# A hybrid decoder step on one core: sample queries, first q/k transposes and softmax steps in other places of the program

## The chip, the core and the metric

The kernel runs on one core of a Trainium2 chip: TensorE (PE in the profile, with PEld for its weight loads), VectorE (DVE), ScalarE (ACT), GpSimd (POOL) and SyncE (SP, which issues most of the DMAs). The metric is the device time of one execution in microseconds (us). Before the change the median of three timed runs is 905.75 us (904.86 to 906.82).

## The reference, cut to what matters

One decoder layer is computed for a prompt of 512 tokens and for 8 samples of one new token each; every sample has 4096 past tokens in a paged cache of 32 pages of 128 tokens. All is in float32.

```python
z = rmsnorm(x, attn_norm_w) @ w_in             # -> q latent, kv latent, rope key, u, v
q = (rmsnorm(q_lat, q_norm_w) @ w_uq).reshape(B, T, 8, 96)
q_nope, q_rope = rmsnorm(q[..., :64]), rope(rmsnorm(q[..., 64:]))
k_nope = rmsnorm(einsum('bkr,rhd->bkhd', c, w_uk), k_nope_norm_w)   # also for every cached token
s = (q_nope . k_nope + q_rope . k_rope) * SCALE                    # causal
o = softmax(s) @ c @ w_uv
u, v = gelu(z_u), gelu(z_v)
sg = u * (tril(w_s) @ v + b_s)                 # per chunk of 128 tokens, 8 groups
h = x + concat([o, sg]) @ w_o
h = h + conv_ffn(rmsnorm(h));  h = h + sigmoid(rmsnorm(h) @ w_ple_gate) * e
```

The normalisation of a cached key needs the sum of squares of its 64 values, so for every page the product `c @ w_uk` (128 tokens by 8 heads by 64) is really computed; the scores of the sample's query come out of the same matmul in 8 more columns (`w_uk` has 2 x 256 columns and 2 x 4 more, which hold the query folded through `w_uk`).

## The kernel before

Nearly all products are float32 in three passes (`mm3`, lines 149 to 151): each operand is split into a high part in a short format (a copy or cast, L138 or L140, on ACT, at times on POOL) and the rest (a subtraction, L133 or L146, on DVE or POOL), and high x high, high x rest and rest x high are added up in PSUM.

The order in which an engine issues its instructions is drawn up when the kernel is built: a scheduler takes them in the order of the program, by what it believes to be ready at each moment, so that a later instruction can stand ahead of an earlier one that it believes to be still waiting. On the chip each engine then keeps that order strictly. `with tc.issue_after(x.ins)` makes the instructions of a block stand behind instruction `x` on its engine. Tiles come from pools with few buffers: `ms` (2 banks of PSUM), `mm` (3 pairs of banks), `G` (10), `A` (8), `W` (9), `WR` (3), `U` (20), and a new tile waits until an old one of its pool has been read for the last time.

The stages, with the times of the profiled execution:

- 0 to 76 us: input norm, the projections to q, kv and u. For each of five token tiles (four of the prompt, t = 0 to 3, and t = 4 with the 8 samples) q and k are normalised and q's 32 rope columns are turned (L470 to L473 and `rope`, L373 to L376), in the order t = 4, 0, 1 on DVE and t = 2, 3 on POOL.
- 76 to 119 us: the products with `w_v` for the five tiles (`v_mm`, 24 matmuls of 512 columns each, order 4, 0, 1, 2, 3), each followed by the gelu on ACT (L520), and the chunk mixing (`mix`): for a prompt tile the split of v, 12 matmuls against the lower-triangular `w_s` (`wsh`, `wsl`, made from `wsr` by L883 and a split), four additions on DVE (L563) and four products on POOL (L567); for the samples' tile two operations on DVE (L542, L543), four small transposes on TensorE (L546) and four products (L548). Into this stage the scheduler has put: the samples' queries: 8 transposes (L484), a scaling (L485), ACT copies into the block-diagonal `qbd` (L506), 8 matmuls through `w_ukT` (L500), the score of the new token (L486 to L494, on 8 partitions of DVE); and the transposes of q and k of the first two prompt heads (L645, four at a time, `t_step`), whose results are split into `G` and `A` tiles.
- 119 to 206 us: attention of the prompt in 16 blocks (`pa_score`, `pa_t`, `pa_out`), with two cache pages of sample 0 in each block.
- 206 to 408 us: the pages of samples 1 to 7. `s_page` takes one page: 6 matmuls of 260 columns in an `mm` tile, the square on ACT (L761), the copy of the raw scores on ACT (L762) and the sum of squares on DVE (L763). Four pages form a group n (n = 0 to 63, eight to a sample); a group is loaded by SP (L605), its rope keys gathered by POOL (L592), and it is split on ACT or POOL (L719) and POOL (L133) two or three groups ahead. The softmax of sample b runs as small `steps` behind given pages of sample b+1. The gated mixture `sgr` is split in four parts behind the groups in `SGS`, high part on ACT, rest on POOL.
- 408 to 906 us: output projection (`o_half`), the convolutional FFN, the gate.

The steps of the softmax before, by the page that they stand behind: 4: variance (L804) and its logarithm; 5: exponential, square; 6: L815; 7: L160 and L161; 8: L817; 9: the maximum (L818); 16: its transpose (L794); 17: L797 and L798; 20: L801, which spreads the maximum by a matmul; 21 to 24: subtraction, exponential, sum; 27: the product with the cached latents (L838); 29: its copy.

Of the kernel before, what the change touches and what calls it, by code (L numbers as in the profile page):

```python
# [7 lines left out]
F32 = mybir.dt.float32  # L8
# [4 lines left out]
AF = mybir.ActivationFunctionType  # L13
# [9 lines left out]
DN = 64  # L23
# [16 lines left out]
NG = 10  # L40
NAT = 8
KRQ = 4
SGS = (51, 54, 59, 62)
EF = 3
PF = 2

# [2 lines left out]
def trunk_step(ctx: ExitStack, tc: tile.TileContext, I, O):  # L49
# [98 lines left out]
    def mm3(out, lh, ll, rh, rl, start, stop):  # L148
        nc.tensor.matmul(out, lh, rh, start=start, stop=False)  # L149
        nc.tensor.matmul(out, lh, rl, start=False, stop=False)  # L150
        return nc.tensor.matmul(out, ll, rh, start=False, stop=stop)  # L151
# [275 lines left out]
    def h96(t, n=128):  # L427
        return t[:n, 0:768].rearrange("p (h d) -> p h d", d=DQ)
# [50 lines left out]

    qs_, ks_ = qtok[4], ktok[4]  # L480
    qgT = const([96, 8, 8], F32, "qgT")
    ps = ms()
    for h in range(8):
        nc.tensor.transpose(ps[:96, h * 8:h * 8 + 8], qs_[:8, h * DQ:(h + 1) * DQ], ident[:8, :8])  # L484
    nc.vector.tensor_scalar(qgT.rearrange("p h b -> p (h b)"), ps[:96, 0:64], gq96[:, 0:1], None, op0=ALU.mult)  # L485
    nc.vector.tensor_mul(h96(ks_, 8)[:, :, 0:DN], h96(ks_, 8)[:, :, 0:DN], gqk8[:, 0:1].to_broadcast([8, 8, DN]))  # L486
    nc.vector.tensor_mul(qs_[:8, 0:768], qs_[:8, 0:768], ks_[:8, 0:768])
    snew = S()
    nc.vector.tensor_reduce(snew[:8, 0:8], h96(qs_, 8), axis=AX.X, op=ALU.add)
    nc.vector.tensor_scalar(snew[:8, 0:8], snew[:8, 0:8], SCALE, None, op0=ALU.mult)  # L490
    snall = const([128, 8, 8], F32, "snall")
    nc.gpsimd.memset(snall, NEG)
    nc.vector.tensor_mul(snall[:8], eye8[:, 0].rearrange("p (b h) -> p b h", b=8), snew[:8, 0:8].unsqueeze(1).to_broadcast([8, 8, 8]))
    nc.vector.tensor_add(snall[:8], snall[:8], eye8[:, 1].rearrange("p (b h) -> p b h", b=8))  # L494

    wukT = WR()
    nc.sync.dma_start(wukT[0:64, 0:1024], I["w_ukT"])
    ps = ms()
    for h in range(8):
        nc.tensor.matmul(ps[:, h * 8:h * 8 + 8], wukT[0:64, h * 128:(h + 1) * 128], qgT[0:64, h], start=True, stop=True)  # L500
    qtil = const([128, 8, 8], F32, "qtil")
    nc.vector.tensor_copy(qtil.rearrange("p h b -> p (h b)"), ps[:, 0:64])
    qbd = const([128, 8, 4, 8], F32, "qbd")
    nc.gpsimd.memset(qbd, 0.0)
    for j in range(4):
        nc.scalar.copy(qbd[32 * j:32 * j + 32, :, j, :], qgT[64:96].rearrange("p h b -> p b h"))  # L506


    bsb = G()
# [7 lines left out]
    def v_out(t, ps):  # L517
        n = TOK[t][1]
        vg[t] = G()
        nc.scalar.activation(vg[t][:n, 0:512], ps, AF.Gelu_apprx_tanh, scale=rtok[:n, t:t + 1])  # L520

    def v_mm(t):
        t0, n = TOK[t]
        sl = slice(t0, t0 + n)
        ps = mm()[:n, 0]
        for j in range(4):
            wh, wl = wget(k_v[j], 3 - j)
            for i in range(2):
                mm3(ps, xh[j][:, i, sl], xl[j][:, i, sl], u3(wh, 2, 512)[:, i], u3(wl, 2, 512)[:, i],
                    j == 0 and i == 0, j == 3 and i == 1)  # L530
        v_out(t, ps)

    def mix(t):
        t0, n = TOK[t]
# [87 lines left out]

    pq_ = {}

    def prep_items(hp):

        qk = [None] * 4
        pq_[hp] = [None, qk]

        def v_step():  # L630
            cs = slice(hp * 128, hp * 128 + 128)
            ps = ms()
            for t in range(4):
                ts_ = slice(t * 128, t * 128 + 128)
                nc.tensor.matmul(ps[:, ts_], ct[:, ts_], wuv[:, cs], start=True, stop=True)
            v = G()
            nc.scalar.copy(v[:, 0:512], ps)
            pq_[hp][0] = v

        def t_step(c, w):  # L640
            h = 2 * hp + c
            src, sc = ((qtok, gq96), (ktok, None))[w]
            ps = ms()
            for t in range(4):
                nc.tensor.transpose(ps[:96, t * 128:(t + 1) * 128], src[t][:, h * DQ:(h + 1) * DQ], ident)  # L645
            th, tl = (A(F32R), A(F32R)) if c else (G(F32R), G(F32R))
            split(th[:96, 0:512], tl[:96, 0:512], ps[:96], scale=None if sc is None else sc[:, 0:1])
            qk[2 * c + w] = (th, tl)

        return [lambda: t_step(0, 0), lambda: t_step(0, 1), lambda: t_step(1, 0), lambda: t_step(1, 1), v_step]  # L650
# [57 lines left out]
    def s_split(n):  # L708
        if n >= 64:
            return  # L710
        b, g = n // 8, n % 8
        pv = pages[b][1][g]
        if n < 12:
            t = U(F32R)
            ch, cl = t[:, 0:512], t[:, 512:1024]
        else:
            ch, cl = A(F32R)[:, 0:512], A(F32R)[:, 0:512]
        raw = pv[:, :, 0:128]
        (nc.gpsimd.tensor_copy if n % 2 else nc.scalar.copy)(u3(ch, 4, 128), raw)  # L719
        subs.append(sub(u3(cl, 4, 128), raw, u3(ch, 4, 128), "g"))  # L720
        csp[n] = (ch, cl)
# [48 lines left out]
    def s_softmax(b):  # L770

        ss, raw, scp = bst[b]
        sc = scp[:, 0:264]
        s3 = sc.rearrange("p (c h) -> p c h", h=8)
        yt = G()
        y0, t = yt[:, 0:256], yt[:, 256:512]
        m1, m2, psum = S(), S(), S()

        def act(*args, **kw):
            with tc.issue_after(squares[-1].ins):  # L780
                exps.append(nc.scalar.activation(*args, **kw))

        bst[b] = (scp, psum)
        hold = {}

        def after_keys(f):

            with tc.issue_after(kmms[-1].ins):
                f()

        def mx_t(after=None):
            hold["t"] = ms()
            with tc.issue_after((after or kmms[-1]).ins):
                nc.tensor.transpose(hold["t"][:8, 0:128], m1[:, 0:8], ident)  # L794

        def mx_all():
            nc.vector.tensor_reduce(m2[:8, 0:1], hold["t"][:8, 0:128], axis=AX.X, op=ALU.max)  # L797
            nc.vector.tensor_scalar(m2[:8, 8:16], ident[:8, 0:8], m2[:8, 0:1], None, op0=ALU.mult)  # L798

        def mx_b():  # L800
            after_keys(lambda: nc.tensor.matmul(hold["t"][:, 128:136], ones[:8], m2[:8, 8:16], start=True, stop=True))  # L801

        def var():
            nc.gpsimd.tensor_scalar(ss, ss, 1.0 / DN, EPS, op0=ALU.mult, op1=ALU.add)  # L804
            act(y0, ss, AF.Ln)

        def rstd():
            act(y0, y0, AF.Exp, scale=-0.5)
            act(t, y0, AF.Square)

        with_qbd[16] = mx_t
        steps.update({
            4: var,
            5: rstd,
            6: lambda: nc.vector.tensor_mul(raw, raw, y0),  # L815
            7: lambda: newton(raw, ss, raw, t),
            8: lambda: nc.vector.tensor_add(sc[:, 0:256], sc[:, 0:256], raw),  # L817
            9: lambda: nc.vector.tensor_reduce(m1[:, 0:8], s3.rearrange("p c h -> p h c"), axis=AX.X, op=ALU.max),  # L818
            17: mx_all,
            20: mx_b,  # L820
            21: lambda: nc.vector.tensor_sub(s3, s3, hold["t"][:, 128:136].unsqueeze(1).to_broadcast([128, 33, 8])),
            23: lambda: act(sc, sc, AF.Exp),
            24: lambda: nc.vector.tensor_reduce(psum[:, 0:8], s3.rearrange("p c h -> p h c"), axis=AX.X, op=ALU.add),
            27: lambda: s_pv(b),
            29: lambda: s_out(b),
        })
# [58 lines left out]
    split(wsh[:, 0:1024], wsl[:, 0:1024], wsr[:, 0:1024])  # L885
    v_mm(0)
    mix(4)
    p0 = prep_items(0)
    p0 = prep_items(0)
    v_mm(1)  # L890
    mix(0)
    p0[0]()
    v_mm(2)
    mix(1)
    p0[1]()
    p0[2]()
    v_mm(3)
    tc.keep_in_program_order(nc.scalar.preload_act_table_set("natural_log_exp_and_others"))
    wuv = G()
    nc.sync.dma_start(wuv[:, 0:512], I["w_uv"])  # L900
    s_load(0)
    s_split(0)
    s_split(1)
    mix(2)
    mix(3)
    p0[3]()
    p0[4]()
    blocks = [(hp, qb) for hp in range(4) for qb in range(4)]
    pa_score(0, 0)
# [360 lines left out]
```

## Time and profile before

| what | us |
|---|---|
| median of three timed runs | 905.75 |
| lowest, highest | 904.86, 906.82 |
| the profiled execution, device time | 907.9 |
| its span in the trace | 906.0 |

The mean granted TensorE clock over the span is 0.989. A page of the profile lists busy times of the engines, then groups of instructions; the timeline lists instructions by start and duration with what ended the idle time before them; the table of waits sums such idle times by who waited for whom; the table of stretches gives busy time and granted clock of chosen intervals. Durations of matmuls overlap, so the start of the next one tells how long one costs.

### The profile page before, as it was taken

How to read it: one execution, taken by the hardware profiler on the slowest of the kernel's cores; microseconds unless marked ns; L12 is line 12 of the kernel's file. 1: busy time of each engine (PE TensorE's matmuls, PEld its weight loads, DVE VectorE, ACT ScalarE, POOL GpSimd, SP SyncE). 2: the span in 40 equal slices, each digit the busy share in tenths (PEclk: the TensorE clock that was granted, in tenths of full speed). 3: DMA queues.
4: the chain of work that ended last, by engine and by line, in shares of the span. 5: the costliest groups of instructions: out<-in, count | busy, mean ns of one | idle time of the engine just before them, and what ended most of it. 6: DMA issues, size and time to landing. Idle time of an engine off the chain costs nothing.

```text
span 906.0 us, 20621 instructions
## 1 busy us (share of the span) xinstructions
PE 884.8 (98%) x7847; PEld 843.4 (93%) x7847; DVE 645.2 (71%) x1093; ACT 503.6 (56%) x1182; POOL 215.0 (24%) x243
## 2 busy tenths in 40 slices
PE   8998999999999999999999999999999999999997
PEld 6896878889999999889999999999999999999997
DVE  6579676668888898796669776337775437766774
ACT  6573368778888888784446443124443224455561
POOL 4004851237777777730000000000000000000000
PEclk9999999999999999999999999999999999999999
DMA  6332160243667664613332222322222322323311
GB/s 220 99 97 82 48 186 1 80 137 98 180 186 214 190 194 135 203 59 110 84 122 88 89 88 75 113 94 94 94 93 71 116 94 83 97 84 100 117 59 60
DMA packets 65347, 100.43 MB, mean 111 GB/s; under 512 B 13841, under 2 KB 47770, under 8 KB 65250
## 3 DMA queue, kind: packets, MB, share of 16 engines
q1 hardware_dynamic: 63202, 94.93, 33.2%
q0 software_dynamic: 2048, 4.20, 1.8%
q8 instruction: 62, 1.02, 0.5%
q14 instruction: 35, 0.29, 0.1%
HBM read 95.95 MB, written 3.15 MB: 109 GB/s over the span
## 4 chain that ended last, share of the span: by engine, by line
PE 77%; DVE 7%; ACT 6%; issue 4%; DMA 3%; SPq 3%; POOL 1%; ACTq 0%; POOLq 0%; DVEq 0%
PE mm L149 23%; PE mm L150 23%; PE mm L151 23%; DVE ss L763 2%; SPq L605 2%; PE ms L838 1%; ACT sq L761 1%; ACT wr L670 1%; PE ms L697 1%; PE ms L149 1%; DMA wr<-w_u 1%; PE ms L151 1%; PE ms L150 1%; DVE wr L673 1%; PE ms L156 1%
## 5 line engine op out<-in xcount | busy, mean ns | idle before, releaser
L149 PE MATMUL mm<-u,w 128*128 128x260 f32 x1392 | 395.2, 284 | 0.1
L151 PE MATMUL mm<-u,w 128*128 128x260 f32 x1392 | 394.7, 284 | 0.0
L150 PE MATMUL mm<-u,w 128*128 128x260 f32 x1392 | 394.1, 283 | 0.0
L150 PEld LDWEIGHTS mm<-u,w 128*128 128x128 f32 x1392 | 263.0, 189 | 0.2
L151 PEld LDWEIGHTS mm<-u,w 128*128 128x128 f32 x1392 | 262.8, 189 | 0.2 <-issue 0.2
L149 PEld LDWEIGHTS mm<-u,w 128*128 128x128 f32 x1392 | 262.5, 189 | 0.5 <-PE mm L151 0.2
L133 DVE TENSOR_TENSOR w<-wr,w 128x1024 fp32r<-128x1024 f32 (+1 forms) x94 | 112.6, 1199 | 106.1 <-issue 54.0
L763 DVE TENSOR_REDUCE ss<-sq 128x8 f32<-128x512 f32 x256 | 166.8, 678 | 26.4 <-ACT sq L761 21.9
L138 ACT CAST w<-wr 128x1024 fp32r<-128x1024 f32 (+1 forms) x94 | 96.5, 1031 | 140.4 <-PE mm L151 127.1
L761 ACT ACTIVATE sq<-mm 128x512 f32<-128x512 f32 x256 | 153.1, 610 | 33.2 <-PE mm L151 18.7
L149 PE MATMUL mm<-wuk,a 128*128 128x260 f32 x416 | 123.4, 297 | 2.5 <-ACT raw L762 2.1
L151 PE MATMUL mm<-wuk,a 128*128 128x260 f32 x416 | 118.4, 285 | 0.0
L150 PE MATMUL mm<-wuk,a 128*128 128x260 f32 x416 | 118.3, 284 | 0.0
L149 PEld LDWEIGHTS mm<-wuk,a 128*128 128x128 f32 x416 | 79.1, 190 | 8.2 <-ACT raw L762 6.3
L150 PEld LDWEIGHTS mm<-wuk,a 128*128 128x128 f32 x416 | 79.1, 190 | 0.0
L151 PEld LDWEIGHTS mm<-wuk,a 128*128 128x128 f32 x416 | 79.0, 190 | 0.0
L592 POOL DMA_INDIRECT wr<-krT,idx x64 | 62.4, 974 | 14.1 <-issue 6.4
L1082 ACT ACTIVATE a<-abuf,cst 128x512 f32<-128x512 f32 x44 | 35.9, 816 | 39.9 <-DVE abuf L1080 38.8
L1083 DVE SCALAR_TENSOR_TENSOR a<-abuf,cst,a 128x512 f32<-128x512 f32 x44 | 33.0, 751 | 25.7 <-ACT a L1082 25.4
L133 POOL TENSOR_TENSOR a<-u,a 128x512 fp32r<-128x512 f32 x34 | 44.2, 1301 | 17.0 <-ACT a L719 15.0
L762 ACT COPY raw<-mm 128x8 f32<-128x8 f32 x256 | 44.5, 174 | 0.0
L138 ACT CAST u<-a 128x520 fp32r<-128x520 f32 x24 | 15.1, 627 | 43.7 <-DVE a L1121 43.3
(307 smaller groups left out, 1324.4 us busy)
## 6 DMA issues: line engine op xcount, KB each, us to landing
wr<-w_ffi SPq DMA_DIRECT2D x44, 512.0 KB
u<-pages SPq DMA_DIRECT2D x152, 128.0 KB
w<-pages SPq DMA_DIRECT2D x104, 128.0 KB
wr<-w_ffo SPq DMA_DIRECT2D x16, 512.0 KB
wr<-w_o SPq DMA_DIRECT2D x8, 512.0 KB
wr<-w_pg SPq DMA_DIRECT2D x8, 512.0 KB
wr<-w_ffo SPq DMA_DIRECT2D x8, 384.0 KB
a<-xT SPq DMA_DIRECT2D x8, 260.0 KB
```

Of the source, the lines that this page charges most:

```text
L133: return (nc.vector if eng == "v" else nc.gpsimd).tensor_sub(dl, src, dh.bitcast(F32))
L138: nc.scalar.copy(dh, src)
L149: nc.tensor.matmul(out, lh, rh, start=start, stop=False)
L150: nc.tensor.matmul(out, lh, rl, start=False, stop=False)
L151: return nc.tensor.matmul(out, ll, rh, start=False, stop=stop)
L592: nc.gpsimd.indirect_dma_start(krT[:, g * 128:(g + 1) * 128], None, I["krT"], bass.IndirectOffsetOnAxis(ap=idx.bitcast(U32)[:, b * 8 + g:b ...
L605: page_dma.append(nc.sync.dma_start(pv[:, j], I["pages"][bass.ds(rs[j], 1)].rearrange("a p f -> (a p) f")))
L761: squares.append(nc.scalar.activation(u3(sq, 2, 256), ps[:, :, 0:256], AF.Square))
L762: nc.scalar.copy(raw[:, c * 8:c * 8 + 8].rearrange("p (a h) -> p a h", a=2), ps[:, :, 256:260])
L763: nc.vector.tensor_reduce(ss[:, c * 8:c * 8 + 8], sq.rearrange("p (h d) -> p h d", d=DN), axis=AX.X, op=ALU.add)
L1082: nc.scalar.activation(c[:, 0:T], a[:, 2:T + 2], AF.Identity, scale=cw[:, m, 2:3], bias=cw[:, m, 3:4])
L1083: nc.vector.scalar_tensor_tensor(c[:, 0:T], a[:, 1:T + 1], cw[:, m, 1:2], c[:, 0:T], op0=ALU.mult, op1=ALU.add)
```

## The change

It touches four places.

1. The 8 query transposes and all that follows from them are put into `s_queries`, called behind `v_mm(1)`; its transposes stand behind the last matmul of that tile on TensorE. The 8 matmuls through `w_ukT` are put into `s_folded`, called behind `v_mm(2)` in the same way. The two fills on POOL and the load of `w_ukT` stay where they were.
2. The first four q and k transposes (`p0[0]` to `p0[3]`) move from between the v tiles to behind `v_mm(3)`; those issued there stand behind its last matmul. `v_mm` now returns that matmul.
3. The four splits of `sgr` move from behind groups 51, 54, 59, 62 to behind 59, 60, 62, 63.
4. The square moves from page 5 to page 6, the two halves of `newton` get a page each, and the addition and the maximum come one page later. L798 becomes a product of two tensors in place of one with a scalar.

```diff
-SGS = (51, 54, 59, 62)
+SGS = (59, 60, 62, 63)
...
     qs_, ks_ = qtok[4], ktok[4]
     qgT = const([96, 8, 8], F32, "qgT")
-    ps = ms()
-    for h in range(8):
-        nc.tensor.transpose(ps[:96, h * 8:h * 8 + 8], qs_[:8, h * DQ:(h + 1) * DQ], ident[:8, :8])
-    nc.vector.tensor_scalar(qgT.rearrange("p h b -> p (h b)"), ps[:96, 0:64], gq96[:, 0:1], None, op0=ALU.mult)
...
+    nc.gpsimd.memset(snall, NEG)
+    nc.gpsimd.memset(qbd, 0.0)
     wukT = WR()
     nc.sync.dma_start(wukT[0:64, 0:1024], I["w_ukT"])
...
+    def s_queries(after):
+
+        ps = ms()
+        with tc.issue_after(after.ins):
+            for h in range(8):
+                nc.tensor.transpose(ps[:96, h * 8:h * 8 + 8], qs_[:8, h * DQ:(h + 1) * DQ], ident[:8, :8])
+        nc.vector.tensor_scalar(qgT.rearrange("p h b -> p (h b)"), ps[:96, 0:64], gq96[:, 0:1], None, op0=ALU.mult)
+        for j in range(4):
+            nc.scalar.copy(qbd[32 * j:32 * j + 32, :, j, :], qgT[64:96].rearrange("p h b -> p b h"))
+        nc.vector.tensor_mul(h96(ks_, 8)[:, :, 0:DN], h96(ks_, 8)[:, :, 0:DN], gqk8[:, 0:1].to_broadcast([8, 8, DN]))
+        nc.vector.tensor_mul(qs_[:8, 0:768], qs_[:8, 0:768], ks_[:8, 0:768])
...
+    def s_folded(after):
+        ps = ms()
+        with tc.issue_after(after.ins):
+            for h in range(8):
+                nc.tensor.matmul(ps[:, h * 8:h * 8 + 8], wukT[0:64, h * 128:(h + 1) * 128], qgT[0:64, h], start=True, stop=True)
+        nc.vector.tensor_copy(qtil.rearrange("p h b -> p (h b)"), ps[:, 0:64])
...
-    def prep_items(hp):
+    def prep_items(hp, after=None):
...
-            for t in range(4):
-                nc.tensor.transpose(ps[:96, t * 128:(t + 1) * 128], src[t][:, h * DQ:(h + 1) * DQ], ident)
+            with ExitStack() as es:
+                if after:
+                    es.enter_context(tc.issue_after(after.ins))
+                for t in range(4):
+                    nc.tensor.transpose(ps[:96, t * 128:(t + 1) * 128], src[t][:, h * DQ:(h + 1) * DQ], ident)
...
-            nc.vector.tensor_scalar(m2[:8, 8:16], ident[:8, 0:8], m2[:8, 0:1], None, op0=ALU.mult)
+            nc.vector.tensor_mul(m2[:8, 8:16], ident[:8, 0:8], m2[:8, 0:1].to_broadcast([8, 8]))
...
-        def rstd():
-            act(y0, y0, AF.Exp, scale=-0.5)
+        def square():
             act(t, y0, AF.Square)
+            nc.vector.tensor_mul(raw, raw, y0)
...
-            5: rstd,
-            6: lambda: nc.vector.tensor_mul(raw, raw, y0),
-            7: lambda: newton(raw, ss, raw, t),
-            8: lambda: nc.vector.tensor_add(sc[:, 0:256], sc[:, 0:256], raw),
-            9: lambda: nc.vector.tensor_reduce(m1[:, 0:8], s3.rearrange("p c h -> p h c"), axis=AX.X, op=ALU.max),
+            5: lambda: act(y0, y0, AF.Exp, scale=-0.5),
+            6: square,
+            7: lambda: nc.vector.scalar_tensor_tensor(t, ss, -0.5, t, op0=ALU.mult, op1=ALU.mult),
+            8: lambda: nc.vector.scalar_tensor_tensor(raw, t, 1.5, raw, op0=ALU.add, op1=ALU.mult),
+            9: lambda: nc.vector.tensor_add(sc[:, 0:256], sc[:, 0:256], raw),
+            10: lambda: nc.vector.tensor_reduce(m1[:, 0:8], s3.rearrange("p c h -> p h c"), axis=AX.X, op=ALU.max),
...
     v_mm(0)
     mix(4)
-    p0 = prep_items(0)
-    p0 = prep_items(0)
-    v_mm(1)
+    v1 = v_mm(1)
+    s_queries(v1)
     mix(0)
-    p0[0]()
-    v_mm(2)
+    v2 = v_mm(2)
+    s_folded(v2)
     mix(1)
-    p0[1]()
-    p0[2]()
-    v_mm(3)
+    v3 = v_mm(3)
...
+    p0 = prep_items(0, v3)
+    p0[0]()
+    p0[1]()
     mix(2)
+    p0[2]()
+    p0[3]()
     mix(3)
-    p0[3]()
     p0[4]()
```

More of the change, by code (lines that the diff above doesn't have):

```diff
@@ L481, in trunk_step @@
     qgT = const([96, 8, 8], F32, "qgT")
-    ps = ms()
-    for h in range(8):
-        nc.tensor.transpose(ps[:96, h * 8:h * 8 + 8], qs_[:8, h * DQ:(h + 1) * DQ], ident[:8, :8])
-    nc.vector.tensor_scalar(qgT.rearrange("p h b -> p (h b)"), ps[:96, 0:64], gq96[:, 0:1], None, op0=ALU.mult)
[L486 to L489, printed above, removed]
@@ L490, in trunk_step @@
-    nc.vector.tensor_scalar(snew[:8, 0:8], snew[:8, 0:8], SCALE, None, op0=ALU.mult)
     snall = const([128, 8, 8], F32, "snall")
+    qtil = const([128, 8, 8], F32, "qtil")
+    qbd = const([128, 8, 4, 8], F32, "qbd")
     nc.gpsimd.memset(snall, NEG)
-    nc.vector.tensor_mul(snall[:8], eye8[:, 0].rearrange("p (b h) -> p b h", b=8), snew[:8, 0:8].unsqueeze(1).to_broadcast([8, 8, 8]))
-    nc.vector.tensor_add(snall[:8], snall[:8], eye8[:, 1].rearrange("p (b h) -> p b h", b=8))
+    nc.gpsimd.memset(qbd, 0.0)
@@ L496, in trunk_step @@
     wukT = WR()
     nc.sync.dma_start(wukT[0:64, 0:1024], I["w_ukT"])
[L498 to L506, printed above, removed]
+    def s_queries(after):
[8 more added lines that the diff above has]
+        nc.vector.tensor_mul(qs_[:8, 0:768], qs_[:8, 0:768], ks_[:8, 0:768])
+        snew = S()
+        nc.vector.tensor_reduce(snew[:8, 0:8], h96(qs_, 8), axis=AX.X, op=ALU.add)
+        nc.vector.tensor_scalar(snew[:8, 0:8], snew[:8, 0:8], SCALE, None, op0=ALU.mult)
+        nc.vector.tensor_mul(snall[:8], eye8[:, 0].rearrange("p (b h) -> p b h", b=8),
+                             snew[:8, 0:8].unsqueeze(1).to_broadcast([8, 8, 8]))
+        nc.vector.tensor_add(snall[:8], snall[:8], eye8[:, 1].rearrange("p (b h) -> p b h", b=8))
@@ L528, in v_mm @@
             for i in range(2):
-                mm3(ps, xh[j][:, i, sl], xl[j][:, i, sl], u3(wh, 2, 512)[:, i], u3(wl, 2, 512)[:, i],
-                    j == 0 and i == 0, j == 3 and i == 1)
+                last = mm3(ps, xh[j][:, i, sl], xl[j][:, i, sl], u3(wh, 2, 512)[:, i], u3(wl, 2, 512)[:, i],
+                           j == 0 and i == 0, j == 3 and i == 1)
         v_out(t, ps)
+        return last
     def mix(t):
```

## The prediction, made before the result was known

> **What bounds the kernel now.** I read the page first, then the waits of TensorE, then the granted clock in short stretches, then the timeline where the change lies.
>
> ```profile
> PE 884.8 (98%) x7847; PEld 843.4 (93%) x7847; DVE 645.2 (71%) x1093; ACT 503.6 (56%) x1182; POOL 215.0 (24%) x243
> ```
>
> TensorE is busy 98% of the span, so the time is its work, plus what it waits, plus what it loses to a lower clock. The gain of any edit must come from the last two. Between 76 us and the first prompt block its longest wait is this one (who waited for whom: total us, times, longest):
>
> ```profile
> PE ms L484 <- DVE u L376: 2.6, 1, 2.6
> ```
>
> In the timeline (start, duration, engine, line) it sits in the middle of the v tiles, which begin at 76.4, and the 16 small matmul records of L500 follow a little later:
>
> ```profile
> 76.38 0.39 PE L149 MATMUL mm<-w,u 128*8 128x512 f32 x1
> ...
> 86.26 0.54 PE L484 MATMUL ms<-cst,u 8*96 8x8 f32 x8 [2.56 <-DVE u L376]
> ...
> 91.73 1.95 PE L500 MATMUL ms<-qgT,wr 64*128 64x8 f32 x16
> ```
>
> The table of stretches (interval, busy, instructions, granted clock, DMA) shows what each costs beyond itself:
>
> ```profile
> 87.40:90.70 3.30, 3.30 (x10) 0.51 0.00 0
> 90.70:94.20 3.50, 3.50 (x24) 0.98 0.03 5
> 94.20:97.50 3.30, 3.30 (x9) 0.51 0.00 0
> 97.60:101.00 3.40, 3.40 (x16) 0.99 0.00 0
> 367.30:370.70 3.40, 3.40 (x16) 0.50 0.64 185
> ```
>
> Behind the wait at 83.7 (16 records in 3.4 us at the full clock, a start every 0.23; 9 or 10 at half), behind L500, and behind a third gap at 365, the clock is halved for about 3.4 us; in each some 1.7 us of work is lost. So the place around L484 costs 2.6 us of waiting and up to 3.4 us of clock: 6.0 us in this execution, the largest sum at one place.
>
> [...]
>
> The third gap lies in the pages, in sample 6:
>
> ```profile
> PE ms L801 <- DVE s L798: 1.9, 1, 1.9
> ```
>
> L798 has 8 elements on 8 partitions. In sample 4 it takes 0.21 us, in sample 6 2.33:
>
> ```profile
> 307.68 0.21 DVE L798 TENSOR_SCALAR s<-cst,s 8x8 f32<-8x8 f32 x1
> 364.62 2.33 DVE L798 TENSOR_SCALAR s<-cst,s 8x8 f32<-8x8 f32 x1
> 364.40 1.31 POOL L133 TENSOR_TENSOR u<-u,u 128x520 fp32r<-128x520 f32 x1
> 365.67 1.25 POOL L133 TENSOR_TENSOR a<-u,a 128x512 fp32r<-128x512 f32 x1
> ```
>
> It ends at 366.95, when POOL's two subtractions end (366.92). The first of them, 520 wide, is a split of `sgr`. The sum of exponentials (L823), which stands at one page of each sample, dates the samples 4 to 7:
>
> ```profile
> 312.21 0.67 DVE L823 TENSOR_REDUCE s<-sc 128x8 f32<-128x264 f32 x1
> 340.26 0.68 DVE L823 TENSOR_REDUCE s<-sc 128x8 f32<-128x264 f32 x1
> 372.55 0.68 DVE L823 TENSOR_REDUCE s<-sc 128x8 f32<-128x264 f32 x1
> 402.42 0.67 DVE L823 TENSOR_REDUCE s<-sc 128x8 f32<-128x264 f32 x1
> ```
>
> The distances are 28.1, 32.3 and 29.9 us: sample 6 costs 4.2 us more than 5, sample 7 1.8 more.
>
> **The queries behind the v tiles.** The 8 transposes and 16 records cost TensorE the same 0.54 and 1.95 us elsewhere. Gone is the wait of 2.56: behind the third v tile (three tiles of 24 matmuls at 0.23 from 76.4: 93.0) L376 has long ended. But DVE stays late. What is late next is the next thing that TensorE takes from DVE, the transposes of `mix(4)` (L546), which need L543. DVE did this:
>
> ```profile
> 85.20 0.67 DVE L472 TENSOR_TENSOR u<-u,g 128x512 f32<-128x512 f32 x1
> ...
> 88.75 0.41 DVE L473 TENSOR_TENSOR u<-u,g 128x256 f32<-128x256 f32 x1
> ...
> 95.53 1.20 DVE L883 TENSOR_TENSOR w<-w,cst 128x1024 f32<-128x1024 f32 x1
> ...
> 98.57 0.96 DVE L543 TENSOR_TENSOR g<-g,cst 8x512 f32<-8x512 f32 x1
> L546 PE MATMUL ms<-cst,g x4: 202/202/224, 101.4 to 101.6; 8*128 8x8 f32 x4
> ```
>
> L543 ended at 99.5; TensorE came to L546 at 101.4 only because of its 6 us of delay. Behind the change L485 to L494 leave this queue, so behind L473 (it ends at 89.15) stand L883 1.20, the four rope operations of tile 1 (half or a quarter as wide as L472: 1.3 together), L542 and L543 (512 wide, 0.67 each, up to 0.96): L543 ends near 93. TensorE, no longer delayed, can reach L546 as soon as the scheduler believes L543 done; it believed the queries ready 2.6 us before they were, so I place L546 around the 15th matmul of `v_mm(1)`, at 90.9. That is a wait of 1.9 to 2.1 us in place of 2.56. Bounds: none, if L546 is placed behind `v_mm(1)`; 5.5, if POOL and DVE alternate as they did from 89 to 99.5 (L543 at 96.4). I take 1.9, by the uncollided rows.
>
> Clock: two halved windows before. L500 is the same low stretch of 1.95 us, and the new wait about as long; I take one window of the two as kept (bounds none and two). Front: 2.56 + 3.4 - 1.9 - 1.7 = **2.4 us less**.
>
> The wait on `v_mm(1)` holds nothing else up: ACT's `qbd` copies and DVE's L486 to L494 come later, but their readers are in the page part, behind the v tiles. `wukT` keeps its buffer until L500, now near 101, and the gathers of POOL, which began at 102.16, need that buffer:
>
> ```profile
> 102.16 1.17 POOL L592 DMA_INDIRECT wr<-krT,idx  x1 [0.24 <-issue]
> ```
>
> They follow POOL's rope without a pause and their readers are the pages, so I cost this at nothing; if the gathers came late enough to hold up page 0, each costs 1.2 us. SP's page loads wait for the `W` tiles of `v_mm(3)` and move with it.
>
> **The q/k transposes behind `v_mm(3)`.** Three of four leave the v stream (three times some 0.55: 1.6 us), and now stand in the tail, where two `ms` buffers let only two through until ACT and DVE have split them:
>
> ```profile
> 117.58 0.69 ACT L520 ACTIVATE g<-mm,rtok 128x512 f32<-128x512 f32 x1 [2.77 <-PE mm L151]
> 118.29 1.28 ACT L898 ACT_TABLE_LOAD   x1
> 118.80 0.60 PE L645 MATMUL ms<-cst,u 128*96 128x128 f32 x4
> 119.00 1.53 DVE L563 TENSOR_TENSOR g<-mm,g 64x256 f32<-64x256 f32 x4 [0.71 <-PE mm L151]
> ...
> 124.76 1.02 DVE L667 TENSOR_REDUCE s<-mm 128x2 f32<-128x256 f32 x2
> ```
>
> From the end of the v tiles (117.5) to the first maximum (L667) it was 7.2 us. Now DVE has there four rests of q and k and one of the mixing (512 wide, 0.7 each) and two L563 groups of 1.53, 6.6 us beginning about 2.6 behind the tiles: 9.2 us, with ACT's gelu, table load and five casts (5 us) beside it. 2.0 us longer against 1.6 saved: **0.4 us more** (bounds -1.6 and +2).
>
> **The splits of `sgr`.** If none lies in sample 6, its excess of 4.2 us goes, half-clock window included. Four high parts on ACT and four rests on POOL then go into sample 7:
>
> ```profile
> L138 ACT CAST u<-u x4: 637/640/642, 355.9 to 377.5; 128x520 fp32r<-128x520 f32 x4
> L133 POOL TENSOR_TENSOR u<-u,u x4: 1305/1315/1327, 356.9 to 378.5; 128x520 fp32r<-128x520 f32 x4
> 408.09 0.22 POOL L1069 MEMSET abuf<- 128x2 f32 x2 [12.49 <-PE mm L150]
> ```
>
> POOL stands idle for the last 12.5 us of sample 7, ACT hardly; two more casts, 1.3 us, half hidden in the pauses, and a collision of 0.5: 1.0 us (bounds 0 and 4.2). **3.2 us less**.
>
> **The steps.** No instruction is added, and DVE's sum is the same. In the trace the scheduler already had the two halves of `newton` behind different pages' L763. I cost it at nothing; a two-input operation that meets POOL costs some 0.3 to 0.5 more (L543 above, 0.96 against 0.67), so one more or one fewer such meeting per sample is 3.5 us over seven samples, either way.
>
> L798 as a product of two tensors: the nearest row is L586, also a two-tensor form with two SBUF inputs of 8 columns.
>
> ```profile
> L586 DVE TENSOR_TENSOR wuk<-qtil,wuk x8: 152/569/1235, 102.8 to 348.2; 128x8 fp32r<-128x8 f32 x8
> ```
>
> It spreads from 0.15 to 1.24, so that form waits for POOL too, and I give the new form no credit. [...]
>
> **The sum.** 2.4 - 0.4 + 3.2 = 5.2 us against the profiled 907.9: 902.7. That execution is 2.15 above the median of 905.75, more than one halved window (1.7): the timed ones probably held fewer of the three, so part of the gain is not theirs to lose. Without windows the parts are 0.7 - 0.4 + 1.5 = 1.8 and for windows I count one and a half (2.5): 4.3 from 905.75 gives 901.5, which I take.
>
> **The rivals.** (a) No new wait: L546 behind `v_mm(1)`, no window in front: 3.6 less, 898. For it: TensorE came to L546 late before; against: L484 was put into the middle of a tile. (b) DVE's lateness shows in full at L546, 5.5 us, and one window in two more: 3.6 + 0.8 worse, 905.9. For it: L543 did end 6.6 us later than L546 would want it; against: half of that was the queries' own operations. (c) The change doesn't do what it says: the splits are hoisted as before (the last of the four, named for sample 7, begins at 378.5, 6 us behind L823 of sample 6) and still meet L798 of sample 6: 3.2 lost, 904.7. Against: the `U` tiles they need compete with page loads that now come first. (d) Slower: the splits fall between page 16 and the end of sample 7. Two rests back to back on L798 cost 1.9 + 1.7 as at 364.6; the last split behind the last page costs 0.64 + 1.32 and a window, 3.7, before `o_half`. 7.3 against the 4.2 of sample 6 and the 2.0 or nothing saved in front is 1.1 to 3.1 slower: 908. It decides from where a rest of 1.3 us ends later than 2 us before L801 or `o_half`. For it: their place in the program; against: POOL's idle 12 us.
>
> **Chances.** Forecast 0.46 (899.5 to 903.9), (a) 0.15, (b) 0.11, (c) 0.14, (d) 0.14. About 0.2%, 1.8 us, can be told from no change. Faster: forecast, (a), and a third of (b) and (c), 0.69; slower: (d), 0.14; same 0.17. The range 896.5 to 907 leaves out half of (d) and the ends of (a) and of the steps.
>
> **What would show it.** Right: no wait at L484, one of about 2 us at L546, one halved window before 110, first L667 two to three us earlier, L823 of samples 5 and 6 28 us apart, L798 at 0.2 in sample 6. Wrong: 520-wide L133 on POOL before 370; L546 waiting above 4 us; a wait at the first `o_half`; samples 2 to 5 not 28.1 us long.

## The result, and the profile after

The changed kernel takes 909.07 us (median of eight runs, 907.01 to 912.29); the kernel before, beside it, 904.97 (902.09 to 907.32). The ratio is 1.0047 with a 95% interval of 1.0033 to 1.0061: the change makes the kernel 3 to 5.5 us slower. The forecast was 901.5, within 896.5 to 907.0; the measured time lies above that range, and the change goes the other way.

The profiled execution of the changed kernel took 910.56 us with a span of 908.7, 1.5 above its median; that of before, with 907.9, lies 2.9 above the median of 904.97. So stages are compared here, not spans. In the changed file the lines named here are 8 to 13 further down; the number before follows once in brackets.

The page's line of busy times is the same as before to some 2 us, with the same counts of instructions, so the loss is again waiting and clock:

```profile
PE 885.0 (97%) x7847; PEld 841.9 (93%) x7847; DVE 646.0 (71%) x1093; ACT 501.5 (55%) x1182; POOL 213.3 (23%) x243
```

The longest waits of TensorE in the changed kernel (who waited for whom: total us, times, longest):

```profile
PE ms L554 <- DVE g L551: 4.1, 1, 4.1
PE mm L149 <- ACT raw L773: 2.7, 7, 0.9
PE mm L259 <- POOL xs L282: 1.9, 2, 1.4
PE mm L149 <- ACT sq L138: 1.8, 1, 1.8
PE ms L805 <- DVE s L830: 1.2, 4, 0.7
```

The wait of 2.56 us at the queries is gone, and so is the one of 1.9 at the maximum in sample 6 (L801 before). In their place stand 4.1 us at the transposes of the samples' mixing (L554, before L546) and 1.8 behind the v tiles (0.9 before). A new entry is L805 (before L794): the transpose of the maximum now waits in four samples. This is what DVE did ahead of L554:

```profile
85.03 1.21 DVE L895 TENSOR_TENSOR w<-w,cst 128x1024 f32<-128x1024 f32 x1
...
86.91 1.52 DVE L499 TENSOR_TENSOR u<-u,cst 8x512 f32<-8x512 f32 x1
...
88.70 1.20 DVE L133 TENSOR_TENSOR wr<-w,wr 128x1024 fp32r<-128x1024 f32 x1
89.83 0.67 DVE L550 TENSOR_TENSOR g<-g,cst 8x512 f32<-8x512 f32 x1
90.43 0.67 DVE L133 TENSOR_TENSOR sq<-g,sq 128x512 fp32r<-128x512 f32 x1
91.03 1.52 DVE L551 TENSOR_TENSOR g<-g,cst 8x512 f32<-8x512 f32 x1
...
92.61 0.41 PE L554 MATMUL ms<-cst,g 8*128 8x8 f32 x4 [4.07 <-DVE g L551]
```

The first v matmul starts at 72.31 in this execution (before: 76.38), so L551 (before L543) ends 20.2 us behind it. Of the queries' operations, the scaling of the new keys (L499, before L486) has not left the queue, and two splits (L133) that stood behind L543 before now stand ahead of L551. The stretches at half clock in this stage (interval; busy time and count of instructions of PE, PEld, DVE, ACT and POOL; clock; DMA):

```profile
93.60:97.00 3.40, 3.40 (x20) 2.90 (x19) 2.04 (x3) 2.39 (x6) 3.40 (x6) 0.50 0.00 0
97.00:100.30 3.30, 3.30 (x11) 2.72 (x11) 2.45 (x7) 0.65 (x2) 2.61 (x5) 0.50 0.00 0
107.40:110.70 3.30, 3.30 (x13) 2.83 (x12) 2.10 (x5) 0.18 (x1) 2.41 (x3) 0.52 0.19 45
121.00:124.30 3.30, 3.30 (x17) 3.27 (x17) 3.08 (x7) 0.58 (x1) 1.70 (x4) 0.51 0.79 228
```

Two follow the wait at L554, one the small matmuls of L512 (before L500), and one the waits in the tail (the part behind the last v tile). That makes four halved windows (stretches of about 3.4 us at half the clock), where before had two. For the pages the sum of exponentials (L835, before L823) dates the samples again:

```profile
287.96 0.67 DVE L835 TENSOR_REDUCE s<-sc 128x8 f32<-128x264 f32 x1
317.16 0.67 DVE L835 TENSOR_REDUCE s<-sc 128x8 f32<-128x264 f32 x1
345.99 0.67 DVE L835 TENSOR_REDUCE s<-sc 128x8 f32<-128x264 f32 x1
374.88 0.67 DVE L835 TENSOR_REDUCE s<-sc 128x8 f32<-128x264 f32 x1
406.52 0.64 DVE L835 TENSOR_REDUCE s<-sc 128x8 f32<-128x264 f32 x1
```

The distances are 29.2, 28.8, 28.9 and 31.6 us. The excess of sample 6 is gone, as forecast (32.3 before, 28.9 now). But an ordinary sample, 28.1 before, now costs 28.9, and sample 7 31.6 in place of 29.9. What happens in an ordinary sample shows in the timeline of sample 4, first before, then after (L817 before and L829 after is the addition of the scores):

```profile
301.26 0.41 DVE L817 TENSOR_TENSOR sc<-sc,raw 128x256 f32<-128x256 f32 x1
...
301.75 1.29 POOL L133 TENSOR_TENSOR a<-u,a 128x512 fp32r<-128x512 f32 x1 [1.09 <-ACT a L719]
```

```profile
305.66 1.29 POOL L133 TENSOR_TENSOR a<-u,a 128x512 fp32r<-128x512 f32 x1 [1.09 <-ACT a L730]
...
305.76 1.47 DVE L829 TENSOR_TENSOR sc<-sc,raw 128x256 f32<-128x256 f32 x1
...
307.92 0.60 ACT L772 ACTIVATE sq<-mm 128x512 f32<-128x512 f32 x1 [1.23 <-DVE ss L774]
...
310.05 0.39 PE L149 MATMUL mm<-wuk,a 128*128 128x260 f32 x1 [0.44 <-ACT raw L773]
```

Before, the addition was through 0.1 us ahead of POOL's subtraction. One page later it begins 0.1 behind the subtraction's start and takes 1.47 us: it ends at 307.23, 0.28 behind POOL's 306.95. Such an overlap of a DVE and a POOL instruction is called a meeting below. The next sum of squares on DVE stands behind the addition, ACT's square waits 1.23 us for a buffer that this sum still reads, and TensorE gets its tile 0.44 late. It is so in every sample from 2 to 6. The other moved steps do not differ: in sample 4 the product before (L815 before, L820 after) takes 0.90 in both kernels, and the two halves of `newton` take 0.92 and 0.41. The group of the addition over the kernel (min/median/max in ns), before and after:

```profile
L817 DVE TENSOR_TENSOR sc<-sc,raw x8: 407/410/1340, 216.0 to 413.1; 128x256 f32<-128x256 f32 x8
```

```profile
L829 DVE TENSOR_TENSOR sc<-sc,raw x8: 409/1464/1471, 220.1 to 417.1; 128x256 f32<-128x256 f32 x8
```

### The profile page after: what moved, and what is told of

Read it like the earlier page. It is cut to its first block, busy times and chain, and to the rows that moved or that the text cites. A ratio compares the mean times of both kernels' runs of the same rounds, so it can differ in the third digit from the quotient of the medians.

```text
span 908.7 us, 20622 instructions
## 1 busy us (share of the span) xinstructions
PE 885.0 (97%) x7847; PEld 841.9 (93%) x7847; DVE 646.0 (71%) x1093; ACT 501.5 (55%) x1182; POOL 213.3 (23%) x243
## 4 chain that ended last, share of the span: by engine, by line
PE 78%; DVE 12%; ACT 6%; issue 2%; DMA 1%; SPq 0%; ACTq 0%; POOLq 0%; DVEq 0%; POOL 0%
PE mm L149 24%; PE mm L151 23%; PE mm L150 23%; DVE ss L774 5%; PE ms L850 2%; ACT wr L681 1%; ACT sq L772 1%; PE ms L708 1%; DVE sc L829 1%; PE ms L149 1%; DVE wr L684 1%; PE ms L151 1%; PE ms L150 1%; DVE g L827 1%; PE ms L156 1%
## 5 line engine op out<-in xcount | busy, mean ns | idle before, releaser
L133 DVE TENSOR_TENSOR w<-wr,w 128x1024 fp32r<-128x1024 f32 (+1 forms) x94 | 112.6, 1199 | 102.7 <-issue 54.0
L149 PEld LDWEIGHTS mm<-wuk,a 128*128 128x128 f32 x416 | 78.3, 188 | 10.6 <-ACT raw L773 7.3
L133 POOL TENSOR_TENSOR a<-u,a 128x512 fp32r<-128x512 f32 x34 | 44.2, 1300 | 19.6 <-ACT a L730 14.9
```

The lines of the kernel that those rows point to most:

```text
L133: return (nc.vector if eng == "v" else nc.gpsimd).tensor_sub(dl, src, dh.bitcast(F32))
```

## The experiments

The theory from this: **the steps** cost 0.8 us in each of samples 2 to 6 through one meeting of DVE and POOL; **the splits** save what was forecast; **the queries** lose, since DVE's queue, not the queries, sets the front (the stage from the first v matmul to the first maximum); **the transposes** add a longer tail. The rivals are the prediction's own steps.

In the table, "first max" is the first maximum of the prompt's attention (L667, after L678); it and the last v matmul are given as distances in us from the first v matmul, start to start. A sample is timed from its first sum of squares to the next sample's, and samples 2 to 5 is the mean of four. Sample 7 has no next one; where it is named, it is given by its first 31 pages (27.8 before, 29.4 changed). The executions of before that stand beside a kernel differ from row to row, so it is the ratio that compares.

| kernel | us | ratio to before (95%) | last v | first max | samples 2 to 5 | sample 6 |
|---|---|---|---|---|---|---|
| before | 904.97 | 1 | 40.8 | 48.4 | 28.1 | 32.3 |
| changed | 909.07 | 1.0047 (1.0033 to 1.0061) | 42.5 | 54.2 | 28.9 | 28.9 |
| s_steps | 908.46 | 1.0032 (1.0019 to 1.0045) | 42.1 | 49.4 | 28.9 | 32.9 |
| s_sgs | 901.38 | 0.9957 (0.9942 to 0.9972) | 42.0 | 49.3 | 28.1 | 28.5 |
| s_front | 907.38 | 1.0027 (1.0014 to 1.0039) | 44.0 | 51.8 | 28.1 | 32.3 |
| s_qk | 905.44 | 1.0003 (0.9991 to 1.0014) | 40.7 | 50.1 | 28.1 | 32.3 |
| a_nosteps | 904.5 | 1.0001 (0.9988 to 1.0014) | 42.4 | 52.0 | 28.1 | 28.5 |
| m_add10 | 905.61 | 1.0012 (0.9999 to 1.0025) | 40.5 | 47.8 | 28.3 | 32.8 |
| m_pool | 902.32 | 0.9973 (0.9962 to 0.9984) | 40.5 | 47.9 | 28.0 | 28.4 |
| a_pool | 906.74 | 1.0023 (1.0008 to 1.0038) | 40.9 | 50.3 | 28.0 | 28.1 |
| f_mix | 904.53 | 1.0001 (0.9989 to 1.0013) | 42.5 | 51.5 | 28.1 | 28.5 |
| f_fill | 907.91 | 1.0039 (1.0023 to 1.0055) | 43.0 | 52.2 | 28.1 | 30.8 |
| f_late | 901.4 | 0.9970 (0.9956 to 0.9983) | 36.6 | 47.1 | 28.1 | 28.5 |
| f_late2 | 901.17 | 0.9956 (0.9940 to 0.9972) | 35.1 | 49.0 | 28.1 | 28.6 |

The front is unchanged in five of these kernels (before, s_steps, s_sgs, m_add10, m_pool), and its first maximum still comes at 47.8 to 49.4; one trace tells such a distance to about 1 us.

**Each part alone, on the kernel before.** s_steps takes the fourth part of the diff, s_sgs the third (`SGS`), s_front the first, s_qk the second.

> Before with only the fourth part of the change (softmax steps, L798 as a product). Theory: the addition of sc and raw (L829 after, L817 before), one page later, meets a subtraction of POOL and takes 1.47 us in place of 0.41, DVE holds up ACT's square and TensorE's next page; samples 1 to 6 cost 28.9 us each in place of 28.1, in all 4 to 5.5 us more than before (ratio 1.0045 to 1.006). Rival: the 0.8 us per sample come from another part (the split places or the queries shift POOL's subtractions against the pages); then this kernel is within 1 us of before and the addition takes 0.41.

> Before with only the third part of the change (the splits of sgr in groups 59, 60, 62, 63). Theory: sample 6 falls from 32.3 to 28.1 us, sample 7 and what follows give back 1 to 2: 2 to 4 us less than before (ratio 0.9955 to 0.998). Rival: what sample 7 gives back is all of it, within 1 us of before.

> Before with only the first part of the change (the samples' queries behind the second and third prompt tile of v; the q and k transposes where they were). Theory: TensorE waits about 4 us at the transposes of the samples' mixing, since DVE has the scaling of k, the split of the triangular weights and a split of v ahead of them, in place of 2.6 at the queries; with one or two halved clock windows more, 1.5 to 5 us more than before. Rival (the step of the prediction): 1 to 3 us less than before.

> Before with only the second part of the change (the first q and k transposes behind the last tile of v). Theory: from the last v matmul to the first maximum 11 to 12 us in place of 7.5, less 1.6 in the v tiles, 2 to 3 us more than before. Rival (the step of the prediction): 0.4 more, within 1 us of before.

By their ratios, of 905 us: steps +2.9 (1.7 to 4.1), splits -3.9 (-5.2 to -2.5), queries +2.4 (1.3 to 3.5), transposes +0.3 (-0.8 to 1.3). The steps' loss is there with nothing else changed:

```profile
L818 DVE TENSOR_TENSOR sc<-sc,raw x8: 407/1462/1506, 215.2 to 413.9; 128x256 f32<-128x256 f32 x8
```

(L818 is the addition in s_steps, m_add10 and m_pool.) So the rival, that the splits or queries shift POOL against the pages, falls. The 4 to 5.5 us of the theory lie above the measured 2.9: sample 1 costs 28.4 there, and not 28.9, since its addition falls beside a gather of POOL (L592) and takes 0.41 us there. For the transposes the prediction's own step held, and the theory's 2 to 3 us fell. The four add up to +1.7, the whole to +4.3.

**The steps taken out of the whole change.** a_nosteps is the changed kernel with the `steps` and L798 of before.

> The changed kernel with the steps of before (parts one to three alone). If the parts add up as measured singly (+2.4, +0.3, -3.9): 903.8, 1.2 us less than before. If the 2.5 us by which the whole change exceeds the sum of its parts lie in front (the first two parts together): about 906.3, with the first maximum 53 us or more behind the first v matmul and sample 7 (its first 31 pages) at 28.4. If they lie in sample 7 (split places and steps together): 903.8 and sample 7 at 28.4, where the whole change has 29.4.

By its ratio it is at +0.1 us (-1.1 to 1.3), midway between the two forecasts of -1.2 and +1.3, so the time alone does not choose between them. The first maximum comes at 52.0, short of the 53 that the front would have needed, and sample 7 takes 28.4 us, where the whole change has 29.4. So the first three parts together save nothing, the fourth adds some 4 us to them, and about 1 us of what the sum of the parts lacks lies in sample 7. In the whole change the last of ACT's four casts of `sgr` (0.64 us) falls into sample 7, in a_nosteps ahead of it, and ACT waits longer for POOL's variance (L815, before L804), which stands behind a rest. First the changed kernel, then a_nosteps:

```profile
385.92 1.32 POOL L133 TENSOR_TENSOR u<-u,u 128x520 fp32r<-128x520 f32 x1
...
387.32 0.41 POOL L815 TENSOR_SCALAR ss<-ss 128x256 f32<-128x256 f32 x1
...
387.76 0.42 ACT L792 ACTIVATE g<-ss 128x256 f32<-128x256 f32 x1 [0.71 <-POOL ss L815]
```

```profile
379.95 1.32 POOL L133 TENSOR_TENSOR u<-u,u 128x520 fp32r<-128x520 f32 x1
...
381.35 0.40 POOL L815 TENSOR_SCALAR ss<-ss 128x256 f32<-128x256 f32 x1
...
381.78 0.42 ACT L792 ACTIVATE g<-ss 128x256 f32<-128x256 f32 x1 [0.43 <-POOL ss L815]
```

This is read from two traces, not tested by itself. What else the sum lacks is within the intervals of the parts.

**Where the addition stands.** m_add10 is s_steps with the addition behind page 10 and the maximum behind 11:

```diff
-            9: lambda: nc.vector.tensor_add(sc[:, 0:256], sc[:, 0:256], raw),
-            10: lambda: nc.vector.tensor_reduce(m1[:, 0:8], ...
+            10: lambda: nc.vector.tensor_add(sc[:, 0:256], sc[:, 0:256], raw),
+            11: lambda: nc.vector.tensor_reduce(m1[:, 0:8], ...
```

> The softmax steps alone as in s_steps, but the addition one page later still (behind page 10 in place of 9) and the maximum behind 11. Theory (POOL's subtraction that begins behind page 9 holds the addition of two SBUF tiles until it ends): behind page 10 POOL gathers and casts, the addition takes 0.41 us again and samples 2 to 5 cost 28.1 us; the time is within 1 us of before, 2 to 4 less than s_steps. Rival (every page later shortens the time up to the maximum's transpose, and that wait is what costs): samples 2 to 5 cost 28.9 or more, the wait for the maximum grows.

```profile
298.38 1.28 POOL L133 TENSOR_TENSOR a<-u,a 128x512 fp32r<-128x512 f32 x1 [1.09 <-ACT a L719]
...
299.07 0.87 DVE L818 TENSOR_TENSOR sc<-sc,raw 128x256 f32<-128x256 f32 x1
```

The addition takes 0.87, not the 0.41 forecast: POOL's subtraction came later than I had it (it waits for ACT's cast), and was not through. The addition ends at 299.94, again 0.28 behind POOL's 299.66. Samples 2 to 5 cost 28.3 us, so a stay shorter by 0.6 gives some 0.55 per sample back. It is not the later page that costs (the rival), but what is left of POOL's instruction. The time is 1.1 us above before (-0.1 to 2.3), where within 1 was forecast: samples 2 to 5 give 0.8 of it, and sample 6 gives 0.5, where the splits still stand and L798 takes 3.08 us.

**The addition on POOL.** m_pool is s_steps, a_pool the changed kernel, with

```diff
-            9: lambda: nc.vector.tensor_add(sc[:, 0:256], sc[:, 0:256], raw),
-            10: lambda: nc.vector.tensor_reduce(m1[:, 0:8], ...
+            9: lambda: nc.gpsimd.tensor_add(sc[:, 0:256], sc[:, 0:256], raw),
+            11: lambda: nc.vector.tensor_reduce(m1[:, 0:8], ...
```

> The steps as in s_steps, but the addition is done by POOL in place of DVE, and the maximum stands behind page 11. Theory (what costs is DVE's stay in the addition, which holds up the sums of squares): samples 2 to 5 cost 27.5 to 28.1 us, since DVE has 0.41 us less to do there; 0 to 4 us less than before. Rival (POOL's addition, 0.7 us or so, delays POOL's splits or stands in the way of DVE's other operations of two tiles): 28.3 us or more per sample.

> The changed kernel with one step altered: the addition of sc and raw is done by POOL, and the maximum stands a page later. Theory (the addition's stay of 1.47 us per sample is what the steps cost, in the whole change as in s_steps): samples 2 to 6 cost 28.0 us in place of 28.9, 903.5 to 905.5, about 4.5 us less than the changed kernel and no slower than before. Rival (with the splits of sgr in sample 7, POOL has no room for it): samples 2 to 6 as forecast but sample 7 at 29.5 or more, 905.5 to 907.

```profile
L818 POOL TENSOR_TENSOR sc<-sc,raw x8: 731/741/744, 214.1 to 406.4; 128x256 f32<-128x256 f32 x8
```

Samples 2 to 5 cost 28.0 us in both. By the ratios, m_pool gains 5.3 us on s_steps and 2.4 (1.4 to 3.4) on before. What it gains on before comes from sample 6: with the splits of `sgr` where they were it is at 28.4 in place of 32.3, and L798 takes 0.18 us there. That meeting is gone because POOL's order is another: the rest of the second split begins at 362.46, 2.7 us behind L798. The expectation did not have that, so this gain is luck. a_pool gains 2.3 us on the changed kernel, not the 4.5 of the theory: samples 2 to 6 give 4.5 back, but sample 1 costs 30.7 in place of 28.5, and sample 7 stays at 29.7, as the rival had it. In sample 1 TensorE waits for the gathered rope keys, and a halved window follows at 221; in m_pool the same wait, without a halved window, makes 29.3. The wait in a_pool:

```profile
221.20 0.34 PE L156 MATMUL ms<-qbd,wr 128*32 128x32 f32 x8 [0.74 <-DMA wr<-krT,idx]
```

**The front: moving the wait.** f_mix is s_front and s_sgs, with `mix(4)` put behind `s_queries(v1)` and its transposes behind `v1`. f_late moves more behind the tile t = 2:

```diff
     v_mm(0)
-    mix(4)
     p0 = prep_items(0)
     v1 = v_mm(1)
     s_queries(v1)
-    mix(0)
-    p0[0]()
     v2 = v_mm(2)
     s_folded(v2)
+    mix(4)
+    mix(0)
+    p0[0]()
     mix(1)
```

> Before with the first and third part, and the mixing of the samples' tile behind the second prompt tile of v and the queries, in place of ahead of that tile. Theory (TensorE waits 4.1 us at its transposes because it comes to them with three matmuls of that tile left, while DVE's queue reaches them 20 us behind the first v matmul): the wait falls to under 1.5 us, and with it a halved window or two: 2 to 4 us less than s_front where the two are alike (first maximum 48 to 50 us behind the first v matmul in place of 51.9); in all 899 to 901.5. Rival (DVE's lateness only moves on to the next thing that TensorE takes from it, the first prompt mixing): a wait of 3 us or more there, 902.5 to 904.

> Before with the first and third part, and both the mixing of the samples' tile and that of the first prompt tile behind the third prompt tile of v (5.5 us of matmuls later than in f_mix). Theory (DVE's queue of the rope, the triangular weights and the splits ends about 20 us behind the first v matmul, whatever the order, and TensorE must have work until then): no wait over 1 us and at most one halved window between the first v matmul and the last, which is at +38 to +40 us in place of +42.5 to +44; 897 to 900.5. Rival (the mixing that is put off comes back behind the last tile, or the waits only move again): 901 to 904, with a wait of 2 us or more named behind the tiles.

In f_mix half of the wait at the samples' mixing (L555) is still there, and the transposes of q and k (L657) wait for POOL's rope next:

```profile
96.98 0.41 PE L555 MATMUL ms<-cst,g 8*128 8x8 f32 x4 [2.10 <-DVE g L551]
...
98.26 0.45 PE L657 MATMUL ms<-cst,u 128*96 128x128 f32 x1 [0.52 <-POOL u L376]
...
99.90 0.45 PE L657 MATMUL ms<-cst,u 128*96 128x128 f32 x1 [1.19 <-POOL u L376]
```

The first maximum comes at 51.5, where s_front has 51.8: nothing was gained. That is the rival, but the waits stand at other places than it named. In f_late the v tiles run through: the last v matmul is at 36.6, some 5 us earlier than in the unchanged front. But the first maximum is at 47.1, 10.6 behind it, where s_sgs has 7.3, and the time is that of s_sgs, in the rival's range. The waits of DVE from 100 to 118 us show why:

```profile
DVE g L571 <- POOL u L575: 6.1, 1, 6.1
```

The additions of the mixing (L571, before L563) wait for POOL's products (L575), which stand behind POOL's gathers. f_late2 therefore does L575 on DVE.

> f_late with the products of the prompt mixing (L575) on DVE in place of POOL. Theory (in f_late the 5 us gained in the v tiles came back behind them: DVE's additions waited 6.1 us for POOL's products, which stood behind POOL's gathers of 1.25 us each): with the products on DVE the additions of the third prompt tile begin some 2.4 us earlier, the first maximum falls from +47.1 to +44.5 to 45.5 us behind the first v matmul, 898 to 900. Rival (ACT's table load and casts, or the gathers themselves, then hold the first maximum): +46.5 or more, 900.5 to 902.

The last v matmul is at 35.1, the first maximum at 49.0: nothing gained again, as the rival had it. TensorE now waits 2.7 us for ACT's split behind the last gelu and a table load (0.9 before), and 0.8 for the load of `w_uv`:

```profile
PE mm L149 <- ACT sq L138: 2.7, 1, 2.7
PE ms L643 <- DMA g<-w_uv: 0.8, 1, 0.8
```

**The clock.** f_fill is s_front with 16 matmuls of 128 x 512 into the `ms` tile of the samples' mixing ahead of its transposes, where TensorE waits.

> s_front with 16 more matmuls of a v tile's size, whose results nothing uses, at the place where TensorE waits 4.1 us for the samples' mixing. Theory (the wait is what halves the clock behind it): 3.7 us of the wait are filled, some 0.4 are left, the halved windows at 95 to 102 are gone or one is left, and the last v matmul is 1.7 to 3.4 us earlier than in s_front (+44.0): 904 to 906. Rival (the small matmuls that follow, L495 and L512, or the time of execution decide about the clock): the halved windows stay, the last v matmul within 0.5 of +44.0, 907 to 908.

The stretches behind the place, s_front first, then f_fill:

```profile
95.60:99.00 3.40, 3.40 (x20) 2.96 (x19) 2.11 (x3) 2.46 (x7) 3.40 (x6) 0.50 0.00 0
99.00:102.30 3.30, 3.30 (x13) 2.48 (x12) 2.45 (x6) 1.26 (x3) 2.61 (x5) 0.50 0.00 0
```

```profile
95.00:98.40 3.40, 3.16 (x25) 2.47 (x25) 2.37 (x7) 2.34 (x6) 3.40 (x5) 1.00 0.04 12
98.40:101.80 3.40, 1.83 (x8) 1.41 (x9) 3.31 (x8) 1.45 (x3) 3.32 (x6) 1.00 0.00 0
```

The clock is 1.00 in both stretches of f_fill and 0.50 in both of s_front, so the wait had halved it: in the changed kernel and a_nosteps, with that wait left in, two stretches at 0.50 follow it as well. The window behind the small matmuls of L512, at 109, stays in f_fill, as the rival had it; over the whole span the mean clock is 0.995, in s_front 0.991. But TensorE is busy for only 1.83 of the second 3.4 us: it waits 1.3 there for POOL's rope. The last v matmul comes 1 us earlier and the first maximum 0.4 later, with a halved window in the tail, and the time is no better (907.9; s_front 907.4). Clock won in front of a late engine was not won.

## Why the prediction was wrong, step by step

**The steps (forecast 0, measured +2.9 alone and some 4 in the whole).** This is the step that failed: "I cost it at nothing; a two-input operation that meets POOL costs some 0.3 to 0.5 more". The prediction put the term at nothing without having read where POOL's subtraction stands; it asked what DVE does at each page, not what POOL does there. Its bound of 3.5 us either way covers the +2.9, but not the 4 of the whole. The price was taken from a mild meeting (L543, 0.96 against 0.67, beside a POOL instruction of 0.47 us). The meeting of the addition cost DVE about what was left of POOL's instruction, 1.06 of its 1.29 us in sample 4; it comes at the same place in samples 2 to 6; and it passes from DVE through ACT's buffers to TensorE (0.8 of the 1.06 us). The row that showed the full price stood in the prediction (L798: 2.33 us, ending with POOL) and was used only for sample 6. Priced as that row shows it, the whole of POOL's instruction, a meeting would have had a bound of some 1.3 us, an estimate from POOL's 1.29 here.

**The queries (forecast -2.4, measured +2.4).** The place was right: the wait at L484 went, and one at L546 came. Two sizes were not right. First, "L485 to L494 leave this queue ... L543 ends near 93", which is 16.6 us behind the first v matmul; it was 20.2. L486 needs no transpose and stayed (1.52), the rest of the triangular weights (1.20) and of the first v tile (0.67) came in ahead, and L543 itself met POOL (1.52 in place of 0.67), as L486 had: twice the same 0.85 that the price of a meeting left out. TensorE came to L546 behind the 21st matmul of the tile, not the 15th. The wait of 4.1 lies between the bounds named (none and 5.5). Second, the clock: one window of two was to remain, and s_front has three. Behind both lies something that the sum did not have: it counted waits and windows as TensorE's own time. f_mix, f_fill, f_late and f_late2 each took such a time away, and each time most or all of it came back at the next thing that TensorE takes from DVE, POOL or ACT. That the late queues set the front is argued from these four kernels; none of them made the queues shorter.

**The windows (counted at 1.7 us each).** The prediction held the profiled execution to be 2.15 us above the median through the three halved windows that it listed, and so counted one and a half of them. That trace has two more, ahead of the v tiles:

```profile
8.90:12.30 3.40, 3.40 (x11) 0.50 1.02 384
36.20:39.60 3.40, 3.40 (x19) 0.51 0.00 0
```

Its first v matmul comes at 76.4 us, in the other thirteen traces at 72.3 to 74.4; so the excess is likely there, not in the windows that the change was to remove. The price was too high as well. Of the 103 executions of before that were timed beside the experiments, 30 had a mean granted clock of 0.995 and a median of 903.4 us, 20 had 0.990 and 905.9. The difference of 0.005 over 904 us is about 2.6 windows, so a window came with about 1 us of time, by this estimate, not 1.7.

**The transposes (forecast +0.4, measured +0.3, -0.8 to 1.3).** Right, and by its reasons: in s_qk the first maximum comes 9.4 us behind the start of the last v matmul, in the five traces of the unchanged front 7.3 to 7.6, so the tail is some 2 us longer, as forecast. In the changed kernel's trace it is 11.7, with a wait of 1.8 for ACT's split and a halved window. That belongs to this execution: a_nosteps and a_pool have the same front, and there it is 9.6 and 9.4, with a wait of 1.0.

**The splits (forecast -3.2, measured -3.9, -5.2 to -2.5).** Right: sample 6 falls from 32.3 to 28.5, sample 7 (first 31 pages) gives 0.6 back, 28.4 against 27.8. That L798 as a product earned no credit was right as well. In the changed kernel, whose sample 6 holds no split, it took 0.14 to 0.15 us in all eight samples; in s_steps, where the splits stand as before, it took 2.38 in sample 6 and again ended with POOL's two subtractions (368.00):

```profile
365.63 2.38 DVE L798 TENSOR_TENSOR s<-cst,s 8x8 f32<-8x8 f32 x1
```

**The rivals.** None was what happened. (b) had the front's mechanism, at less than its price. (d) named 908 us, near the measured 909, but that is luck: its reason, splits that cost more in sample 7 than they save, is refuted by s_sgs (-3.9). No rival ended on the slower side through the steps, since a meeting was priced at 0.5 at most. Of the prediction's own signs of being wrong, two came: L546 waited above 4 us, and samples 2 to 5 were not 28.1 us long.

Four versions are faster than before, by 2.4 to 4 us: s_sgs (the third part alone, 901.4), m_pool (902.3), f_late and f_late2. The last two contain the third part, and are no faster than s_sgs without the work on the front.

## What to carry to other kernels

Before a DVE operation with two inputs in SBUF is moved to another place in a loop, read what POOL runs at that place, and price a meeting at the whole of what is left of POOL's instruction (1.06 us here, of 1.29), times the loop, until the timeline shows less. Where three engines are behind in a stage, a wait or a slow clock on the fourth is not a sum to be earned: undo it on paper and ask whose result comes next; only what shortens the late queue, or takes an operation out of it, counts. A step that fits in the middle rounds of a loop can fail in the first and last, where the neighbours differ (samples 1 and 7 here).

## What the runs showed of the hardware

The addition of 256 columns, a DVE operation with two inputs in SBUF, ended 0.28 or 0.29 us behind the subtraction of POOL that it met, however long it had been held: in all such meetings in the two kernels (it took 0.91 to 1.47 us), and in those read in s_steps (at 300.81, 1.47) and m_add10 (at 299.07, 0.87). Operations of 512 columns ended 0.54 us behind a product of POOL's rope (L499 and L551 in the changed kernel, 1.52). These ends are the operation's own 0.41 and 0.67 us less 0.13. Beside a gather of POOL, in sample 1 of the changed kernel, the addition began during one and took 0.41.

The mean clock of the profiled executions changes between kernels in which the front is the same: 0.989 (before), 0.995 (s_steps), 0.992 (s_sgs), 0.994 (m_add10), 0.995 (m_pool); in the 103 executions of before it went from 0.989 to 0.997. The traces of before and of the changed kernel show a pattern in this. In each, all halved windows begin at whole multiples of 3.413 us from one another (before: 8.93, 36.24, 87.44, 94.26, 367.33, 903.22; changed: 93.50, 96.91, 107.15, 120.81, 905.87). If these two traces are cut into such intervals, and the time without a matmul is added up in each whole one that ran at the full clock, then seven hold 1.86 to 2.52 us of it, and all seven were followed by a halved one; the next two, with 1.59 and 1.55 (at 4.75 and 86.67 in the changed kernel), were not. Of the other four halved windows one stands straight behind another (96.91); the intervals ahead of the other three hold small matmuls: 1.95 us of L500 (L512 after) in two, with no time without a matmul, and in one 1.17 us of L341 with 1.05 us without (before, at 32.82). A wait of 2.4 us at L484 stands in s_qk and in s_steps alike, and their mean clocks are 0.989 and 0.995. This pattern is read from two traces, not tested; that the wait of 4.1 us halved the clock, and that filling it removed both windows, is what f_fill shows (1.00 in both stretches, 0.50 in s_front).

POOL's operations, too, were drawn out, as far as its rough spans tell: the same 512-wide product of the rope took 1.22 us before, at 90.03, where DVE's operations were the ones drawn out (L374, 128 wide, 1.13 us, against 0.27 elsewhere), and 4.16 in the changed kernel, where DVE's came one behind another:

```profile
87.85 4.16 POOL L472 TENSOR_TENSOR u<-u,g 128x512 f32<-128x512 f32 x1
```
